# Decoder trunk on one core: two load queues ordered by need at the start, the norm gains on ScalarE's queue, and the last tile's scaling on VectorE

## The chip, the cores and the metric

The kernel runs on one core of one Trainium2 chip. The metric is the time of the device in microseconds (us); lower is better. Engines are named as the profile names them: PE is TensorE, DVE is VectorE, ACT is ScalarE, POOL is GpSimd, SP is SyncE. SP only issues transfers (DMAs); ACT and POOL have queues for transfers of their own.

## What is computed

A decoder trunk of two layers over 512 tokens of width 1024, all in fp32. Layer 0 mixes with a short gated convolution, layer 1 with sliding-window attention; each is followed by a SwiGLU feed-forward part (FFN) of width 2816. Every part ends with a residual update of a normalised result.

```python
def rmsnorm(x, g):
    r = lax.rsqrt(jnp.mean(x * x, axis=-1, keepdims=True) + EPS)
    return (x * r) * g

def short_conv_mixer(h, w_in, conv_w, w_out):
    b_gate, c_gate, u = jnp.split(h @ w_in, 3, axis=-1)
    return (b_gate * causal_depthwise_conv3(c_gate * u, conv_w)) @ w_out

def swiglu(h, w_gate_up, w_down):
    g, u = jnp.split(h @ w_gate_up, 2, axis=-1)
    return (jax.nn.silu(g) * u) @ w_down

# layer 0:  mix = short_conv_mixer(rmsnorm(h, a_pre_norm), w_in, conv_w, w_out)
#           h = h + rmsnorm(mix, a_post_norm)
# layer 1:  mix = window attention of rmsnorm(h, b_pre_norm) @ b_w_q, with k, v of rmsnorm(h, kv_norm)
#           h = h + rmsnorm(mix, b_post_norm)
# both:     h = h + rmsnorm(swiglu(rmsnorm(h, ffn_pre_norm), w_gate_up, w_down), ffn_post_norm)
```

## The kernel before

**Splitting.** TensorE multiplies fp32 numbers as pairs of a high and a low part. ACT copies a tile into its rounded high part (`xhi`, `whi`, `yhi`), DVE subtracts it from the tile for the low part (`xlo`, `wlo`, `ylo`), and each product is three matmuls: high by low, high by high, low by high (`mm3`, L192 to L194). A weight tile is of 128 x 1024; it is loaded by SP into one of seven buffers `raw`, split, and used.

**Order of the work.** Nearly all the work stands in blocks whose order on the engines is written out by hand (`manual_schedule`). The string `CONV` (L37) orders the products of the convolution: `c2 u2 b2` are the three projections of feature tile 2, `P1` to `P7` products of a block scheme for the output, `w0` to `w3` the tiles of the output weights that the closing uses. `in_line` prepares the weights three jobs ahead of their use, and after a job takes steps from a list `late`, the steps that follow a projection on the other engines (L764 to L787). POOL also issues transfers that add blocks of later weights in DRAM (`issue`, L534, tiles `hsum`); each waits for room on POOL's queue, and POOL does its own arithmetic in order with them.

**The start.** `gt` holds all gains that are used as a column per feature, 128 x 64. POOL issues its load (L137). `xt[0]` to `xt[7]` are the transposed input, 128 x 512 each, `first[0]` to `first[2]` the first three weight tiles, which come in three cuts (`CUTS`: feature tiles 0 and 1, then 2 and 3, then 4 to 7) by `piece(queue, t, c)` (L219 to L221). The first two cuts are of 128 KB, the third is of 256 KB, an `xt` of 256 KB. While they come, PE runs ten matmuls on a constant (`idle`). Then ACT does `token_hi(0)` (L674: `xhi` of `xt[0]` times a gain from `gt`) and six pieces of the first weights (`first_hi`, L666), DVE the low parts, and PE the products of feature tile 0 (L686, `pcub`: `products(0, ...)`, nine matmuls with tiles 0, 1, 2 in turn), then those of tiles 1 to 7.

**Close of the convolution.** `close` (L869) makes the output of each of four token tiles in two halves (`pmix`): for tile 0 first all products but the last, and after each half ACT and DVE split two weight tiles of the FFN (`ahead.one()`, L407 and L412). The last product needs the last `yhi` (L775), which comes from the convolution's last projection `b7`. `res` is an `Update` for the norm behind it: `take` adds `pmix` to the tile `mix`, `square_mix` sums the squares on ACT, `mean` makes `uv` on DVE (L292) and `ur`, its power -0.5, on POOL (L296); `scale` multiplies `mix` by the gains `G` (L289, half a tile at a time), and `update` adds it to the residual `h` (L301). Behind it tiles are normalised on ACT (`xn`, L323) and transposed on PE (`xt`, L334). `G` is one row of 1024 gains spread over all partitions, loaded by `res.load` (L253 to L255) on ACT's queue.

**The end.** The loop at L1169 closes the last FFN. The second half of the last token tile is made in two quarters (`take_quarter`, L267): DVE adds `pmix` to `mix` (L270); for the first quarter ACT then sums the squares; for the second DVE adds the sums so far and EPS (`us`, L276), then reduces the quarter's squares into `uv` (L279), and POOL makes `ur` (L283). The first half of `mix` is scaled on POOL, the second on DVE. Two updates of 512 columns each then make the output, with a transfer behind each.

Of the kernel before, what the change touches and what calls it, by code (L numbers as in the profile page):

```python
# [13 lines left out]
ALU = mybir.AluOpType  # L14
# [5 lines left out]
KT = D // P  # L20
# [40 lines left out]
EPS = 1e-6  # L61
# [3 lines left out]
G_FPRE = (24, 32)  # L65
# [3 lines left out]
B_CONV, B_ATT, B_FFN = 0, 1, (2, 3)  # L69
# [3 lines left out]
def yoco_kernel(  # L73
# [22 lines left out]
    nc = tc.nc  # L96
# [39 lines left out]
    gt = const.tile([P, N_GAIN], F32, name="gt")  # L136
    nc.gpsimd.dma_start(gt, gains)  # L137
    ident = const.tile([P, P], F32, name="ident")
# [80 lines left out]
    def piece(queue, t, c):  # L219
        c = slice(CUTS[c][0] * P, CUTS[c][1] * P)  # L220
        queue.dma_start(first[t][:, c], w_in[0, t, :, c])  # L221

    for t in range(3):
        piece(nc.scalar, t, 0)
    nc.sync.dma_start(xt[0], xT[0])
    nc.sync.dma_start(xt[1], xT[1])
    for t in range(2):
        piece(nc.scalar, t, 1)
    nc.sync.dma_start(xt[2], xT[2])
    piece(nc.sync, 2, 1)  # L230
    nc.sync.dma_start(xt[3], xT[3])
# [7 lines left out]
    class Update:  # L239
# [27 lines left out]
        def take_quarter(self, t, c, ps):  # L267

            m = self.mix[t][:, S + c : S + c + 256]
            nc.vector.tensor_tensor(out=m, in0=ps[:, :256], in1=m, op=ALU.add)  # L270
            i = 2 * t
            if not c:
                nc.scalar.activation(self.junk[:, S : S + 256], m, AF.Square, scale=1 / 32,
                                     accum_out=self.s[:, 8:9])
                return
            nc.vector.tensor_scalar(out=self.s[:, i : i + 1], in0=self.s[:, i : i + 1],  # L276
                                    scalar1=self.s[:, 8:9], scalar2=EPS, op0=ALU.add,
                                    op1=ALU.add)
            nc.vector.tensor_tensor_reduce(out=self.junk[:, S : S + 256], in0=m, in1=m,  # L279
                                           scale=1 / D, scalar=self.s[:, i : i + 1],  # L280
                                           op0=ALU.mult, op1=ALU.add,
                                           accum_out=self.v[:, t : t + 1])
            nc.gpsimd.tensor_tensor(out=self.r[:, t : t + 1], in0=self.v[:, t : t + 1],  # L283
                                    in1=mhalf[:, :1], op=ALU.pow)

        def scale(self, t, half, eng=nc.vector):
            c = slice(half * S, (half + 1) * S)
            m = self.mix[t][:, c]
            eng.tensor_tensor(out=m, in0=m, in1=self.G[:, c], op=ALU.mult)  # L289

# [448 lines left out]
    ys, acts, mix_c = [], [], [None] * NB  # L739
    both = []  # L740

    def conv(f, pc=None, pu=None, pb=None):
# [36 lines left out]
        def end():  # L779
            if f >= KT // 2:  # L780
                return [split]
            if f % 2 == 0:
                return []
            p = pair_sums(both[-1], acts)
            return [lambda i=i: (p[i](), p[i + 1]()) for i in (0, 2, 4)]
# [163 lines left out]

    res = Update(mix_c, B_CONV, [G_FPRE[0]])  # L950
    res.leaves = True

    sum_on("o0")
    issue(len(issues))
    ahead = Ahead(first_weights(0))
    with tc.manual_schedule(engines=ALL):
        sum_on("o1")
        issue(len(issues))
        res.load(nc.scalar)
        close(ws, ys, 0, res, ahead)  # L960


    def ffn(l, before, ahead, gain, gpres, following):
# [204 lines left out]
        with tc.manual_schedule(engines=ALL):  # L1168
            for t in range(NB):  # L1169
                for half in range(2):  # L1170
# [8 lines left out]
                    else:  # L1179
# [4 lines left out]
                        if t == NB - 1:  # L1184
                            res.update(t - 1, 0, S)
                            res.scale(t, 0, nc.gpsimd)
                if t < NB - 1:
                    res.scale(t, 0)
                    res.mean(t)
# [404 lines left out]
```

## Time and profile before

| what | value |
|---|---|
| time, median of 3 runs | 1031.55 us (1031.83, 1031.44, 1031.55) |
| time of the profiled execution | 1034.99 us |
| its span in the trace | 1033.2 us |
| PE busy | 1019.7 us, 99% |
| DVE busy | 823.5 us, 80% |
| ACT busy | 576.9 us, 56% |
| POOL busy | 196.7 us, 19% |
| HBM read and written | 237.15 and 102.76 MB, 329 GB/s |

All times inside the kernel come from the one profiled execution, in us from the start of its span. The time of the execution holds 1.8 us more than the span. A row of the timeline gives the start, the length, the engine, the line, the operation with what it writes and reads, how many instructions it joins, and in brackets the idle time ahead of it and what ended that. PE is close to fully busy, so the reading goes to the few places where it stands still or runs at a lower granted clock.

### The profile page before, as it was taken

How to read it: one execution, taken by the hardware profiler on the slowest of the kernel's cores; microseconds unless marked ns; L12 is line 12 of the kernel's file. 1: busy time of each engine (PE TensorE's matmuls, PEld its weight loads, DVE VectorE, ACT ScalarE, POOL GpSimd, SP SyncE). 2: the span in 40 equal slices, each digit the busy share in tenths (PEclk: the TensorE clock that was granted, in tenths of full speed). 3: DMA queues.
4: the chain of work that ended last, by engine and by line, in shares of the span. 5: the costliest groups of instructions: out<-in, count | busy, mean ns of one | idle time of the engine just before them, and what ended most of it. 6: DMA issues, size and time to landing. Idle time of an engine off the chain costs nothing.

```text
span 1033.2 us, 17488 instructions
## 1 busy us (share of the span) xinstructions
PE 1019.7 (99%) x6650; PEld 928.4 (90%) x6650; DVE 823.5 (80%) x1403; ACT 576.9 (56%) x1039; POOL 196.7 (19%) x261
## 2 busy tenths in 40 slices
PE   8999999999999999999999999999999999999997
PEld 7888887999989899999898888889998999989986
DVE  5676657888777978878869998688886788887786
ACT  7232534865655454566466777668565554645632
POOL 0433132102101021000122664221111010210001
PEclk9999999999999999999999999999999999999998
DMA  9797789548978889879503879985899676988732
GB/s 338 282 242 239 187 258 326 170 164 249 315 251 271 269 275 300 282 211 307 196 1 127 220 208 269 265 258 164 257 291 319 182 252 204 315 290 257 249 127 82
DMA packets 66756, 244.59 MB, mean 237 GB/s; under 512 B 7776, under 2 KB 8672, under 8 KB 54896
## 3 DMA queue, kind: packets, MB, share of 16 engines
q1 hardware_dynamic: 51040, 145.52, 38.7%
q0 software_dynamic: 14624, 96.51, 36.5%
q10 hardware_dynamic: 1008, 1.44, 0.4%
q8 instruction: 52, 0.85, 0.3%
q14 instruction: 32, 0.26, 0.1%
HBM read 237.15 MB, written 102.76 MB: 329 GB/s over the span
## 4 chain that ended last, share of the span: by engine, by line
PE 89%; DVE 4%; DMA 4%; ACT 1%; issue 1%; POOL 1%; POOLq 0%; DVEq 0%; ACTq 0%
PE gx L194 7%; PE gx L193 7%; PE gx L192 7%; PE gz L194 4%; PE gz L193 4%; PE gz L192 4%; PE px L193 3%; PE px L192 3%; PE px L194 3%; PE pcub L194 3%; PE pcub L192 3%; PE pcub L193 3%; DMA hsum<-in_w_gb_dram 3%; PE pmix L192 2%; PE pmix L193 2%; PE pmix L194 2%
## 5 line engine op out<-in xcount | busy, mean ns | idle before, releaser
L466 DVE TENSOR_TENSOR wlo<-raw,whi 128x1024 fp32r<-128x1024 f32 x225 | 275.1, 1226 | 93.4 <-ACT whi L465 93.3
L465 ACT ACTIVATE whi<-raw 128x1024 fp32r<-128x1024 f32 x225 | 234.2, 1049 | 120.2 <-DVE raw L453 22.3
L192 PE MATMUL gx<-xt,whi 128*128 128x256 f32 x480 | 135.8, 283 | 0.0
L193 PE MATMUL gx<-xt,whi 128*128 128x256 f32 x480 | 135.8, 283 | 0.0
L194 PE MATMUL gx<-xt,wlo 128*128 128x256 f32 x480 | 135.8, 283 | 0.0
L534 POOL DMA_DIRECT2D hsum<-in_w_gb_dram x96 | 63.4, 728 | 156.3 <-ACT whi L465 82.3
L192 PEld LDWEIGHTS gx<-xt,whi 128*128 128x128 f32 x480 | 92.2, 192 | 0.0
L193 PEld LDWEIGHTS gx<-xt,whi 128*128 128x128 f32 x480 | 92.2, 192 | 0.0
L194 PEld LDWEIGHTS gx<-xt,wlo 128*128 128x128 f32 x480 | 92.2, 192 | 0.0
L534 POOL DMA_DIRECT2D hsum<-hsum x32 | 25.3, 790 | 265.2 <-ACT whi L465 156.0
L1012 ACT ACTIVATE st<-gx 128x256 f32<-128x256 f32 x80 | 30.1, 382 | 81.1 <-PE gx L194 81.0
L193 PE MATMUL pcub<-xhi,whi 128*128 128x512 f32 x168 | 65.4, 389 | 0.0
L192 PE MATMUL pcub<-xlo,whi 128*128 128x512 f32 x168 | 65.4, 389 | 0.0
L194 PE MATMUL pcub<-xhi,wlo 128*128 128x512 f32 x168 | 65.4, 389 | 0.0
L192 PE MATMUL px<-wlo,ahi 128*128 128x512 f32 x120 | 46.7, 389 | 0.0
L193 PE MATMUL px<-whi,ahi 128*128 128x512 f32 x120 | 46.7, 389 | 0.0
L194 PE MATMUL px<-whi,alo 128*128 128x512 f32 x120 | 46.7, 389 | 0.0
L194 PE MATMUL gy<-xhi,wlo 128*128 128x256 f32 x160 | 45.3, 283 | 0.0
L193 PE MATMUL gz<-xt,whi 128*128 128x256 f32 x160 | 45.3, 283 | 0.0
L194 PE MATMUL gx<-xhi,wlo 128*128 128x256 f32 x160 | 45.3, 283 | 0.0
L192 PE MATMUL gy<-xlo,whi 128*128 128x256 f32 x160 | 45.3, 283 | 0.0
L193 PE MATMUL gy<-xhi,whi 128*128 128x256 f32 x160 | 45.3, 283 | 0.0
(270 smaller groups left out, 3123.0 us busy)
## 6 DMA issues: line engine op xcount, KB each, us to landing
hsum<-in_w_gb_dram POOLq DMA_DIRECT2D x96, 512.0 KB, 8.1
raw<-hsum SPq DMA_DIRECT2D x88, 512.0 KB, 7.8
raw<-in_w_gb_dram SPq DMA_DIRECT2D x60, 512.0 KB, 7.8
hsum<-in_w_dn_dram POOLq DMA_DIRECT2D x36, 512.0 KB, 8.6
raw<-in_w_dn_dram SPq DMA_DIRECT2D x32, 512.0 KB, 6.7
hsum<-hsum POOLq DMA_DIRECT2D x28, 512.0 KB, 5.7
raw<-in_w_in_dram SPq DMA_DIRECT2D x21, 512.0 KB, 7.9
hsum<-in_w_dn_dram POOLq DMA_DIRECT2D x12, 768.0 KB, 12.5
```

Of the source, the lines that this page charges most:

```text
L192: nc.tensor.matmul(out, whi, xlo, start=start, stop=False, **kw)
L193: nc.tensor.matmul(out, whi, xhi, start=False, stop=False, **kw)
L194: nc.tensor.matmul(out, wlo, xhi, start=False, stop=stop, **kw)
L465: self.begun = nc.scalar.activation(hi[:, :n], raw, AF.Copy)
L466: nc.vector.tensor_tensor(out=lo[:, :n], in0=raw, in1=hi[:, :n].bitcast(F32), op=ALU.subtract)
L534: nc.gpsimd.dma_start(dst, src, max_dma_last_dim=4 * 4 * S, **kw))
L1012: nc.scalar.activation(s, x, AF.Copy)
```

## The change

Three places are edited.

1. The load of `gt` moves from POOL's queue to the head of ACT's. The loads of the first tiles are issued in another order, and on other queues: ACT keeps `gt` and the first cuts of weight tiles 0 and 1; all the rest is SP's.
2. The `Update` object of the convolution (`res`) is made before the convolution's jobs, and the load of its gains `G` becomes a step in the list `late` behind the split of feature tile 6 (`f == KT - 2`), inside the block of the convolution, in place of the head of the closing's block.
3. In the last FFN's closing, the first half of the last token tile is scaled by DVE behind the second quarter, as the second half already was, and no longer by POOL. In `take_quarter` the small addition for `us` goes ahead of the addition of `pmix` to `mix`.

```diff
--- before.py
+++ after.py
@@ -134,7 +134,6 @@
 
 
     gt = const.tile([P, N_GAIN], F32, name="gt")
-    nc.gpsimd.dma_start(gt, gains)
     ident = const.tile([P, P], F32, name="ident")
     make_identity(nc, ident)
     ones = const.tile([P, P], F32, name="ones")
@@ -220,14 +219,15 @@
         c = slice(CUTS[c][0] * P, CUTS[c][1] * P)
         queue.dma_start(first[t][:, c], w_in[0, t, :, c])
 
+    nc.scalar.dma_start(gt, gains)
+    nc.sync.dma_start(xt[0], xT[0])
+    piece(nc.scalar, 0, 0)
+    piece(nc.sync, 2, 0)
+    piece(nc.scalar, 1, 0)
+    nc.sync.dma_start(xt[1], xT[1])
     for t in range(3):
-        piece(nc.scalar, t, 0)
-    nc.sync.dma_start(xt[0], xT[0])
-    nc.sync.dma_start(xt[1], xT[1])
-    for t in range(2):
-        piece(nc.scalar, t, 1)
+        piece(nc.sync, t, 1)
     nc.sync.dma_start(xt[2], xT[2])
-    piece(nc.sync, 2, 1)
     nc.sync.dma_start(xt[3], xT[3])
     for t in range(3):
         piece(nc.sync, t, 2)
@@ -267,15 +267,16 @@
         def take_quarter(self, t, c, ps):
 
             m = self.mix[t][:, S + c : S + c + 256]
+            i = 2 * t
+            if c:
+                nc.vector.tensor_scalar(out=self.s[:, i : i + 1], in0=self.s[:, i : i + 1],
+                                        scalar1=self.s[:, 8:9], scalar2=EPS, op0=ALU.add,
+                                        op1=ALU.add)
             nc.vector.tensor_tensor(out=m, in0=ps[:, :256], in1=m, op=ALU.add)
-            i = 2 * t
             if not c:
                 nc.scalar.activation(self.junk[:, S : S + 256], m, AF.Square, scale=1 / 32,
                                      accum_out=self.s[:, 8:9])
                 return
-            nc.vector.tensor_scalar(out=self.s[:, i : i + 1], in0=self.s[:, i : i + 1],
-                                    scalar1=self.s[:, 8:9], scalar2=EPS, op0=ALU.add,
-                                    op1=ALU.add)
             nc.vector.tensor_tensor_reduce(out=self.junk[:, S : S + 256], in0=m, in1=m,
                                            scale=1 / D, scalar=self.s[:, i : i + 1],
                                            op0=ALU.mult, op1=ALU.add,
@@ -283,10 +284,10 @@
             nc.gpsimd.tensor_tensor(out=self.r[:, t : t + 1], in0=self.v[:, t : t + 1],
                                     in1=mhalf[:, :1], op=ALU.pow)
 
-        def scale(self, t, half, eng=nc.vector):
+        def scale(self, t, half):
             c = slice(half * S, (half + 1) * S)
             m = self.mix[t][:, c]
-            eng.tensor_tensor(out=m, in0=m, in1=self.G[:, c], op=ALU.mult)
+            nc.vector.tensor_tensor(out=m, in0=m, in1=self.G[:, c], op=ALU.mult)
 
         def mean(self, t):
             nc.vector.tensor_scalar(
@@ -738,6 +739,8 @@
         nc.vector.tensor_scalar(out=nsnk, in0=snk, scalar1=-1.0, scalar2=None, op0=ALU.mult)
     ys, acts, mix_c = [], [], [None] * NB
     both = []
+    res = Update(mix_c, B_CONV, [G_FPRE[0]])
+    res.leaves = True
 
     def conv(f, pc=None, pu=None, pb=None):
 
@@ -778,7 +781,7 @@
 
         def end():
             if f >= KT // 2:
-                return [split]
+                return [split, lambda: res.load(nc.scalar)] if f == KT - 2 else [split]
             if f % 2 == 0:
                 return []
             p = pair_sums(both[-1], acts)
@@ -947,16 +950,12 @@
         return ([w_gu[l, f, j] for f in range(2) for j in range(2)]
                 + [w_gb[l, 0, b] for b in range(2)])
 
-    res = Update(mix_c, B_CONV, [G_FPRE[0]])
-    res.leaves = True
-
     sum_on("o0")
     issue(len(issues))
     ahead = Ahead(first_weights(0))
     with tc.manual_schedule(engines=ALL):
         sum_on("o1")
         issue(len(issues))
-        res.load(nc.scalar)
         close(ws, ys, 0, res, ahead)
 
 
@@ -1183,9 +1182,8 @@
                         res.square_mix(t, half)
                         if t == NB - 1:
                             res.update(t - 1, 0, S)
-                            res.scale(t, 0, nc.gpsimd)
+                res.scale(t, 0)
                 if t < NB - 1:
-                    res.scale(t, 0)
                     res.mean(t)
                 res.scale(t, 1)
                 if t < NB - 2:
```

In the rows below, a name such as `raw_108` is a tile with its buffer number; the numbers differ between the two kernels (`raw_108` before is `raw_107` after: weight tile 0). First, ACT at the start of the program, before:

```order
L221 DMA raw_108<-in_w_in_dram 128x256
L221 DMA raw_109<-in_w_in_dram 128x256
L221 DMA raw_110<-in_w_in_dram 128x256
L221 DMA raw_108<-in_w_in_dram 128x256
L221 DMA raw_109<-in_w_in_dram 128x256
L659 ACT_TABLE_LOAD
L659 ACTIVATE warm_256<-ones 128x1
L674 ACTIVATE xhi_222<-xt_104,gt 128x512
L666 ACTIVATE whi_240<-raw_108 128x128
L666 ACTIVATE whi_242<-raw_109 128x128
L666 ACTIVATE whi_244<-raw_110 128x128
```

The same place of ACT after the change:

```order
L222 DMA gt<-in_gains_dram 128x64
L220 DMA raw_107<-in_w_in_dram 128x256
L220 DMA raw_108<-in_w_in_dram 128x256
L660 ACT_TABLE_LOAD
L660 ACTIVATE warm_256<-ones 128x1
L675 ACTIVATE xhi_222<-xt_103,gt 128x512
L667 ACTIVATE whi_240<-raw_107 128x128
L667 ACTIVATE whi_242<-raw_108 128x128
L667 ACTIVATE whi_244<-raw_109 128x128
```

ACT issues three transfers in place of five ahead of its table load, and the first of them is `gt`. SP's first transfers before (`xt_104` is the pair of `xt[0]` and `xt[1]`, `xt_105` that of `xt[2]` and `xt[3]`):

```order
L225 DMA xt_104<-in_xT_dram 128x512
L226 DMA xt_104<-in_xT_dram 128x512
L229 DMA xt_105<-in_xT_dram 128x512
L221 DMA raw_110<-in_w_in_dram 128x256
L231 DMA xt_105<-in_xT_dram 128x512
L221 DMA raw_108<-in_w_in_dram 128x512
L221 DMA raw_109<-in_w_in_dram 128x512
L221 DMA raw_110<-in_w_in_dram 128x512
```

And after:

```order
L223 DMA xt_103<-in_xT_dram 128x512
L220 DMA raw_109<-in_w_in_dram 128x256
L227 DMA xt_103<-in_xT_dram 128x512
L220 DMA raw_107<-in_w_in_dram 128x256
L220 DMA raw_108<-in_w_in_dram 128x256
L220 DMA raw_109<-in_w_in_dram 128x256
L230 DMA xt_104<-in_xT_dram 128x512
L231 DMA xt_104<-in_xT_dram 128x512
L220 DMA raw_107<-in_w_in_dram 128x512
L220 DMA raw_108<-in_w_in_dram 128x512
```

The first cut of weight tile 2 (`raw_109` after) now stands between `xt[0]` and `xt[1]`, and the second cuts of all three ahead of `xt[2]`.

Second, ACT at the end of the convolution and the start of its closing, before (L181: halves of the output weights `w1` to `w3`; L465: weights of the last job; L775: the `yhi` of feature tiles 6 and 7; L407: the FFN's weights):

```order
L181 ACTIVATE whi_1306<-raw_1190 128x512
L181 ACTIVATE whi_1307<-raw_1190 128x512
L465 ACTIVATE whi_1344<-raw_1192 128x1024
L775 ACTIVATE yhi_1348<-bry_1132 128x512
L181 ACTIVATE whi_1378<-raw_1194 128x512
L181 ACTIVATE whi_1379<-raw_1194 128x512
L181 ACTIVATE whi_1391<-raw_1216 128x512
L181 ACTIVATE whi_1392<-raw_1216 128x512
L255 DMA G_1451<-in_behind_dram 128x1024
L775 ACTIVATE yhi_1429<-bry_1318 128x512
L407 ACTIVATE whi_1465<-raw_1439 128x1024
L407 ACTIVATE whi_1471<-raw_1441 128x1024
```

The same place after:

```order
L778 ACTIVATE yhi_1319<-bry_1135 128x512
L466 ACTIVATE whi_1351<-raw_1195 128x1024
L255 DMA G_1355<-in_behind_dram 128x1024
L180 ACTIVATE whi_1384<-raw_1197 128x512
L408 ACTIVATE whi_1465<-raw_1442 128x1024
L180 ACTIVATE whi_1385<-raw_1197 128x512
L408 ACTIVATE whi_1471<-raw_1444 128x1024
L180 ACTIVATE whi_1397<-raw_1219 128x512
L408 ACTIVATE whi_1486<-raw_1469 128x1024
L180 ACTIVATE whi_1398<-raw_1219 128x512
L408 ACTIVATE whi_1492<-raw_1475 128x1024
L778 ACTIVATE yhi_1435<-bry_1325 128x512
```

The load of `G` passes the halves of the last two output weights, and the four conversions of the FFN's weights (L407 before, L408 after) now stand between those halves, ahead of the last `yhi`. DVE's subtractions behind them move alike. The order of PE's instructions is the same in both kernels.

Third, DVE at the end of the program, before (`mix_8949` is the last token tile):

```order
L259 TENSOR_TENSOR mix_8949<-pmix_11496,mix_8949 128x512
L301 TENSOR_SCALAR h_11384<-mix_8939,ur_11376,h_11384 128x512
L270 TENSOR_TENSOR mix_8949<-pmix_11513,mix_8949 128x256
L301 TENSOR_SCALAR h_11384<-mix_8939,ur_11376,h_11384 128x512
L270 TENSOR_TENSOR mix_8949<-pmix_11530,mix_8949 128x256
L276 TENSOR_SCALAR us_11374<-us_11374 128x1
L279 ISA junk_11378,uv_11375<-mix_8949,us_11374 128x256
L279 ISA uv_11375 128x1
L289 TENSOR_TENSOR mix_8949<-mix_8949,G_11377 128x512
L301 TENSOR_SCALAR h_11386<-mix_8949,ur_11376,h_11386 128x512 x2
```

And after:

```order
L259 TENSOR_TENSOR mix_8949<-pmix_11496,mix_8949 128x512
L302 TENSOR_SCALAR h_11384<-mix_8939,ur_11376,h_11384 128x512
L275 TENSOR_TENSOR mix_8949<-pmix_11512,mix_8949 128x256
L302 TENSOR_SCALAR h_11384<-mix_8939,ur_11376,h_11384 128x512
L272 TENSOR_SCALAR us_11374<-us_11374 128x1
L275 TENSOR_TENSOR mix_8949<-pmix_11529,mix_8949 128x256
L280 ISA junk_11378,uv_11375<-mix_8949,us_11374 128x256
L280 ISA uv_11375 128x1
L290 TENSOR_TENSOR mix_8949<-mix_8949,G_11377 128x512 x2
L302 TENSOR_SCALAR h_11386<-mix_8949,ur_11376,h_11386 128x512 x2
```

The scaling of 128x512 stands twice on DVE, and the addition for `us` (L272 after) stands ahead of the second quarter's `mix`. POOL has one scaling of 128x512 fewer.

## The prediction

> **What bounds the kernel now.** I read the busy times first, then what TensorE (PE) waited for, then the granted clock in short windows, then the three places that the change touches.
>
> ```profile
> PE 1019.7 (99%) x6650; PEld 928.4 (90%) x6650; DVE 823.5 (80%) x1403; ACT 576.9 (56%) x1039; POOL 196.7 (19%) x261
> PE xt L334 <- ACT xn L323: 2.2, 1, 2.2
> PE pcub L686 <- ACT whi L666: 2.0, 1, 2.0
> ```
>
> The first row is the busy time of each engine, the others are PE's waits (total, times, longest). PE is busy for 99% of the span. Apart from its first wait for a constant it stands still twice: 2.0 us before its first real product (`pcub`), and 2.2 us in the closing of the convolution, where the transposes wait for a normalised token tile. An edit can thus save only at PE's start, at that second stop, after PE's last matmul, or where PE runs slowly. The last is seen in windows of 3.41 us (columns: the stretch, its length, busy time of PE, PEld, DVE, ACT, POOL with counts, granted clock, DMA share, GB/s):
>
> ```profile
> 3.96:7.37 3.41, 1.38 (x11) 1.16 (x10) 0.43 (x3) 2.06 (x7) 0.00 (x0) 1.00 1.07 371
> 7.37:10.79 3.42, 3.42 (x10) 2.77 (x9) 3.17 (x10) 3.42 (x10) 0.00 (x0) 0.50 0.94 287
> 178.04:181.45 3.41, 1.41 (x7) 0.89 (x5) 2.61 (x6) 3.35 (x7) 1.12 (x2) 1.00 1.02 425
> 181.46:184.87 3.41, 3.23 (x16) 3.23 (x16) 2.74 (x5) 1.55 (x4) 0.34 (x1) 0.50 0.90 370
> ```
>
> In both places a window with PE busy for only 1.38 or 1.41 us (40%) is followed by one at clock 0.50. So each stop costs twice: the standing still, and half of the next 3.4 us.
>
> **Part 1, the first loads.** ACT converts the first token tile (`xhi`, which needs the gains `gt` and `xt`), then the six first weight tiles; PE follows.
>
> ```profile
> 0.74 2.37 ACTq L221 DMA_DIRECT2D raw<-in_w_in_dram  x5
> 1.29 0.74 POOL L137 DMA_DIRECT2D gt<-in_gains_dram  x1 [0.84 <-POOLq L1583]
> 4.44 0.20 ACT L659 ACTIVATE warm<-ones 128x1 f32<-128x1 f32 x1
> 5.99 0.72 ACT L674 ACTIVATE xhi<-xt,gt 128x512 fp32r<-128x512 f32 x1 [1.34 <-DMA gt<-in_gains_dram]
> 6.61 1.29 ACT L666 ACTIVATE whi<-raw 128x128 fp32r<-128x128 f32 x6
> 6.96 1.32 PE L686 MATMUL pcub<-xhi,whi 128*128 128x512 f32 x3 [2.03 <-ACT whi L666]
> 10.63 0.93 PE L686 MATMUL pcub<-xhi,whi 128*128 128x512 f32 x3
> 12.75 0.84 PE L686 MATMUL pcub<-xhi,whi 128*128 128x512 f32 x3
> ```
>
> And the times from issue to landing (last number) of the first, second and third transfer on the queues:
>
> ```profile
> xt<-in_xT_dram SPq DMA_DIRECT2D x1, 256.0 KB, 3.5
> raw<-in_w_in_dram ACTq DMA_DIRECT2D x1, 128.0 KB, 3.6
> raw<-in_w_in_dram ACTq DMA_DIRECT2D x1, 128.0 KB, 4.6
> xt<-in_xT_dram SPq DMA_DIRECT2D x1, 256.0 KB, 4.9
> raw<-in_w_in_dram ACTq DMA_DIRECT2D x1, 128.0 KB, 5.1
> gt<-in_gains_dram POOLq DMA_DIRECT2D x1, 32.0 KB, 4.7
> ```
>
> ACT is ready at 4.64 and waits until 5.99 for `gt`, which POOL issued at 1.29 and which took 4.7 us. Issued first on ACT's queue at 0.74, `gt` is of 32 KB; the nearest rows are the first transfers of the two queues, 3.5 and 3.6 us, and its own 4.7 us is the other end. That gives 4.2 to 5.4; I take 4.2, the row of the same queue and rank. `xt` lands there too. So `xhi` runs from 4.2 to 4.9, with the table load and `warm` over by then: three issues end near 2.2 in place of 3.1, and 1.28 us of table load and 0.2 follow.
>
> The next thing that ACT needs is not `gt`. It takes the weight tiles in the order 0, 1, 2, and tile 1 is now ACT's third transfer. Before, the third ones landed at 6.5 (SP: 1.65 + 4.9) and 6.7 (ACT: 1.66 + 5.1), with 1152 KB in all (3 x 256 and 3 x 128). Now the three of SP hold 256, 128, 256 KB and those of ACT 32, 128, 128, which is 928 KB. The second pair ended at 5.7 with 768 KB, so by bytes 928 KB are in at 5.7 + (160 / 384) x 1.0 = 6.1. By rank alone it stays at 6.7. I take 6.0 to 6.1, nearer to the bytes. The second weight conversion, which began one fifth of a us after 6.61, at 6.8, then begins at 6.05: **0.8 us earlier**. From there ACT runs without a gap as before, and its later loads do not come later: the two queues carry the same bytes, 32 KB moved apart. On SP's queue the pieces of the second cut now pass `xt[2]` and `xt[3]`; ACT reads them in just that order, the cut first.
>
> The Trainium skill ("DMA: Bandwidth & Descriptors", Queues, rings and completion order) says that a DMA engine takes turns between queues packet by packet; the trace agrees in that equal ranks landed together, 6.5 and 6.7, though one was twice as large. By that rule alone the sum would lose its 0.8 us, which is the third rival below.
>
> PE follows ACT. If the clock still falls to 0.50, PE does its first 18 matmuls at the same slow pace and the whole is 0.8 earlier. If it does not, more is won: before, the eight or so matmuls from 7.6 to 10.6 stood 0.43 us apart, later nine stand from 10.63 to 12.75, 0.23 apart. VectorE's corrections still hold up some of these, so I count 1.5 us for it, with 1.7 (half of 3.41) as its bound. Whether the clock falls: PE now stops from 4.9 to 5.2, does one product, and stops from 5.5 to 6.4; the rest of the window of 3.41 us is busy, some 64%. The rows show 40% as too little and 100% as enough, and nothing between.
>
> The Trainium skill ("TensorE: Matmul & The Clock Gate", Part 1) has the clock fall after a whole idle window of about 3.4 us. The rows above speak against it: 40% busy was already too little. By that rule the new start would run at full clock; it is the case of the first two rivals, and the rows bear it out only as far as its length of window.
>
> **Part 2, the gains `G` and the close of the convolution.** The load of `G` itself saves nothing: the first row is its issue, and of the transfers issued in this stretch (last number of the two rows behind it: from issue to landing) the slowest took 16.3 us, which would still have `G` in by 163.6, before its use near 168.
>
> ```profile
> 147.26 0.33 ACTq L255 DMA_DIRECT2D G<-in_behind_dram  x1
> raw<-in_w_gu_dram SPq DMA_DIRECT2D x1, 512.0 KB, 8.2
> hsum<-in_w_gb_dram POOLq DMA_DIRECT2D x2, 512.0 KB, 16.3
> 158.97 0.69 DVE L770 TENSOR_TENSOR bry<-pcub,rrow 128x512 f32<-128x512 f32 x1 [0.72 <-PE pcub L194]
> 160.42 0.63 ACT L775 ACTIVATE yhi<-bry 128x512 fp32r<-128x512 f32 x1 [10.46 <-DVE bry L771]
> 162.04 4.63 DVE L412 TENSOR_TENSOR wlo<-raw,whi 128x1024 fp32r<-128x1024 f32 x4 [0.26 <-ACT whi L407]
> 168.82 0.21 DVE L292 TENSOR_SCALAR uv<-us 128x1 f32<-128x1 f32 x1
> 168.27 2.28 POOL L534 DMA_DIRECT2D hsum<-in_w_dn_dram  x4
> 170.30 0.86 POOL L296 TENSOR_TENSOR ur<-uv,mhalf 128x1 f32<-128x1 f32 x1
> 181.64 3.41 PE L334 MATMUL xt<-ident,xn 128*128 128x128 f32 x15 [2.19 <-ACT xn L323]
> ```
>
> What does move is the order on ACT and VectorE: the four conversions of the next stage's weights (4.63 us on VectorE) now stand among the last ones of the convolution. The fourth waits until PE has finished product b7 (158.97 is VectorE's start behind it), and the last `yhi` stands behind it on ACT. I put the rows' durations in the new order: conversion 159.0 to 160.05, its correction on VectorE to 161.5, `bry` to 162.1, `yhi` to 162.75 in place of 161.05. PE needs it after 18 products from 158.97, at 163.05, so some 0.3 us of cover are left; I cost it at nothing, and 0.5 us if the cover goes.
>
> In exchange VectorE reaches tile 0 about 2.5 us earlier. That buys nothing by itself: `uv` was ready at 169.03, but POOL computed `ur` only at 170.30, behind its sum transfers. Those are paced by the DMA queue, whose load is the same, so `ur`, the normalised tile and PE's second stop stay where they are with regard to the convolution: 0, with 1.27 us (170.30 less 169.03) of loss or gain as the bound.
>
> **Part 3, the last tile.** POOL's scaling of 1.30 us goes, and one of 0.69 us comes on VectorE.
>
> ```profile
> 1024.64 1.30 POOL L289 TENSOR_TENSOR mix<-mix,G 128x512 f32<-128x512 f32 x1 [1.54 <-ACT junk L264]
> 1023.66 0.74 DVE L301 SCALAR_TENSOR_TENSOR h<-mix,ur,h 128x512 f32<-128x512 f32 x1
> 1024.83 1.66 DVE L301 SCALAR_TENSOR_TENSOR h<-mix,ur,h 128x512 f32<-128x512 f32 x1
> 1025.60 0.28 PE L194 MATMUL pmix<-whi,alo 128*128 128x256 f32 x1
> 1026.40 0.41 DVE L270 TENSOR_TENSOR mix<-pmix,mix 128x256 f32<-128x256 f32 x1
> 1026.97 0.48 DVE L279 CUSTOM_DVE_ANT_0 junk<-mix,us 128x256 f32<-128x256 f32 x1
> 1027.54 1.05 POOL L283 TENSOR_TENSOR ur<-uv,mhalf 128x1 f32<-128x1 f32 x1 [1.61 <-DVE uv L279]
> 1027.50 0.69 DVE L289 TENSOR_TENSOR mix<-mix,G 128x512 f32<-128x512 f32 x1
> 1028.63 1.41 DVE L301 SCALAR_TENSOR_TENSOR h<-mix,ur,h 128x512 f32<-128x512 f32 x2 [0.44 <-POOL ur L283]
> ```
>
> The same update takes 0.74 us alone and 1.66 us while POOL scales. Without POOL it ends at 1025.57, and the last `mix` waits for PE's last matmul instead (1025.60 + 0.28): 1025.95 in place of 1026.40. The sum `us` now stands ahead of `mix`, so the reduction follows at 1026.4 (before: 1026.97). POOL's `ur` runs 0.57 later, from 1026.95 to 1028.0. VectorE meanwhile scales both halves, two starts 0.6 apart from 1026.9, to 1028.1. The final update begins at 1028.1 in place of 1028.63: **0.5 us less**. If the update stays at 1.66 the second scaling costs about 0.1; if `ur` speeds up, nothing more is won, VectorE being the later one. Bounds: 0.1 more to 0.7 less.
>
> **The sum.** 0.8 + 0 + 0.5 = 1.3 us less. The rows come from a profiled execution of 1034.99 us, with a span of 1033.2; the median of the runs shown is 1031.55, and I take the difference off that: **1030.2 us**. With the bounds of these parts it is 1029.2 to 1031.2.
>
> **Rivals.** *The clock holds at the start, the second stop stays as it is:* 0.8 + 1.5 + 0.5 = 2.8 less, 1028.7. For it: 64% against 40% busy. Against it: nothing shows what is enough, and the position of the windows may differ from run to run.
>
> *It holds at both places:* if PE comes 2.3 us earlier and the windows stay where they are, the second stop, of 2.19 us up to 181.64, becomes one from 177.15 to 179.34 and is cut by the window's edge at 178.04 into 0.9 and 1.3 us, 26% and 38% idle, like the start. Then 1.7 more is won: 4.5 less, 1027.0.
>
> *Landing by rank:* tile 1 of the weights still comes at 6.7, and the start gains 0.1. Then 0.6 less, 1031.0.
>
> *Slower:* the fourth conversion also waits for its own load, and that now holds up the convolution's last `yhi`. It has cover until 159.3; before, its own load (8.2 us, issued at 144.35) landed at 152.5, but the two sum transfers issued near 150.2 took 16.3 and came near 166.5. If this load came then, the last `yhi`, 3.75 later (159.0 to 162.75 above), would stand at 170.25 and PE would stop for 7.2 us from 163.05 instead of 2.2 at 179: a loss of 5.0 less the 1.3 is 3.7, 1035.3. It decides only if that load comes 7 us later than it did.
>
> **How the numbers follow.** Chances: forecast 0.42, clock held at the start 0.22, at both 0.16, landing by rank 0.13, slower 0.07. The forecast is the likeliest, not a mean. The range from 1026.8 to 1031.4 takes in the first four and leaves out the fifth and their ends. A measurement of this kernel tells 0.2%, 2.1 us, from no change; the forecast and the landing by rank lie within it, and the two cases of the held clock are faster by more, with a small part of the forecast's own range: faster 0.43, same 0.50, slower 0.07.
>
> **What would show it.** In the profile after, ACT's first `xhi` begins near 4.2 and its second weight conversion near 6.05; PE's first product stands near 5.2. The window that holds the second and third product shows clock 0.50 next or not, which separates the forecast from the first two rivals. In the close, the last `yhi` stands near 162.7 less the gain, PE has no new wait there, and `ur` still follows POOL's transfers. At the end the update is 0.74 long and the final one begins 0.5 us earlier after PE's last matmul. The forecast is wrong if the clock holds, if PE waits for the last `yhi`, or if tile 1 lands at 6.7.

## The result and the profile after

The changed kernel took 1030.49 us (median of 21 executions, 1028.96 to 1033.39), the kernel before, beside it on the same chips, 1033.34 us (21 executions, 1031.33 to 1037.57). The ratio is 0.9974 with a 95% interval of 0.9963 to 0.9985, so 2.7 us less (1.5 to 3.8). Put on the 1031.55 us from which the forecast started, that is 1028.9 us. The forecast was 1030.2, with 1026.8 to 1031.4 as its range: the sign and the range held, the size was about half of what came. A second comparison, of 11 executions with 29, gave 0.9983 (0.9974 to 0.9993), 1.8 us less.

Executions of the same kernel before differ by 6 us among themselves, and a single trace is one of them. So each reading below says of which execution it is, and the three places are read one by one.

**The start, changed kernel.** The timeline of ACT:

```profile
0.75 0.41 ACTq L222 DMA_DIRECT2D gt<-in_gains_dram  x1
3.89 0.72 ACT L675 ACTIVATE xhi<-xt,gt 128x512 fp32r<-128x512 f32 x1 [0.24 <-DMA gt<-in_gains_dram]
4.64 0.31 ACT L667 ACTIVATE whi<-raw 128x128 fp32r<-128x128 f32 x1
6.76 1.11 ACT L667 ACTIVATE whi<-raw 128x128 fp32r<-128x128 f32 x5 [1.82 <-DMA raw<-in_w_in_dram]
```

The third transfers on the two queues, from issue (1.66) to landing in the last column:

```profile
xt<-in_xT_dram SPq DMA_DIRECT2D x1, 256.0 KB, 4.9
raw<-in_w_in_dram ACTq DMA_DIRECT2D x1, 128.0 KB, 5.1
```

The gains arrive early and the first token tile is converted at 3.89 in place of 5.99, 0.3 us sooner than forecast. But the second weight conversion begins at 6.76 (before: 6.8): it now waits for its own tile, and in this execution the third transfers take the same 4.9 and 5.1 us as before. What PE waited for, and PE in three of the clock's windows, two at the start and the one of the second stop (the columns are those of the prediction's windows; no granted clock was recorded before the first rise, at 10.63, and the view shows that time as 1.00):

```profile
PE xt L335 <- ACT xn L324: 2.5, 1, 2.5
PE pcub L687 <- ACT whi L667: 1.0, 1, 1.0
```

```profile
0.39:3.80 3.41, 2.74 (x13) 2.74 (x14) 0.32 (x3) 1.49 (x2) 0.56 (x4) 1.00 0.56 149
3.80:7.21 3.41, 2.41 (x11) 1.90 (x10) 0.40 (x2) 1.48 (x5) 0.00 (x0) 1.00 1.04 304
177.87:181.28 3.41, 1.60 (x8) 1.05 (x6) 2.67 (x7) 2.96 (x7) 0.58 (x2) 1.00 1.02 425
```

The clock's pace is seen in the products. The first row is of this trace, the second of another execution of the same kernel (`e_after`), whose clock had risen at 5.15:

```profile
8.14 1.05 PE L687 MATMUL pcub<-xhi,wlo 128*128 128x512 f32 x2
```

```profile
7.38 0.62 PE L687 MATMUL pcub<-xhi,wlo 128*128 128x512 f32 x2
```

Two matmuls take 1.05 us in the one and 0.62 in the other: the same program runs the start at half clock in one execution and at full clock in the next. In the one, `close` begins at 158.78 us, in the other at 156.88.

**The close of the convolution, changed kernel** (ACT, DVE, POOL and PE):

```profile
161.71 0.63 ACT L778 ACTIVATE yhi<-bry 128x512 fp32r<-128x512 f32 x1 [1.89 <-DVE bry L774]
166.00 0.21 DVE L293 TENSOR_SCALAR uv<-us 128x1 f32<-128x1 f32 x1
166.31 0.80 POOL L535 DMA_DIRECT2D hsum<-in_w_gb_dram  x1 [15.19 <-DMA hsum<-in_w_gb_dram]
168.11 0.79 POOL L535 DMA_DIRECT2D hsum<-in_w_gb_dram  x1 [1.01 <-DMA hsum<-in_w_gb_dram]
168.63 2.28 POOL L535 DMA_DIRECT2D hsum<-in_w_dn_dram  x4
170.65 0.85 POOL L297 TENSOR_TENSOR ur<-uv,mhalf 128x1 f32<-128x1 f32 x1
171.54 1.29 DVE L302 SCALAR_TENSOR_TENSOR h<-mix,ur,h 128x1024 f32<-128x1024 f32 x1 [4.74 <-POOL ur L297]
182.01 1.86 PE L335 MATMUL xt<-ident,xn 128*128 128x128 f32 x15 [2.53 <-ACT xn L324]
```

The last `yhi` comes 1.3 us later (161.71, before 160.42), under PE's cover. `uv` begins 2.8 us earlier (166.00 for 168.82), and DVE then stands for 4.74 us, since POOL's `ur` still comes behind its sum transfers, at 170.65 (before 170.30). The rows of POOL show why: the first two of these wait for the landing of earlier transfers, until 166.31 and 168.11. PE's second stop remains, 2.53 us.

**The end, changed kernel** (DVE, POOL and PE's last matmul):

```profile
1023.62 0.74 DVE L302 SCALAR_TENSOR_TENSOR h<-mix,ur,h 128x512 f32<-128x512 f32 x1
1024.28 0.21 DVE L272 TENSOR_SCALAR us<-us 128x1 f32<-128x1 f32 x1
1024.40 0.28 PE L193 MATMUL pmix<-whi,alo 128*128 128x256 f32 x1
1024.71 0.42 DVE L275 TENSOR_TENSOR mix<-pmix,mix 128x256 f32<-128x256 f32 x1 [0.22 <-PE pmix L193]
1025.58 1.29 DVE L290 TENSOR_TENSOR mix<-mix,G 128x512 f32<-128x512 f32 x2
1025.74 0.93 POOL L284 TENSOR_TENSOR ur<-uv,mhalf 128x1 f32<-128x1 f32 x1 [3.86 <-DVE uv L280]
1026.79 1.41 DVE L302 SCALAR_TENSOR_TENSOR h<-mix,ur,h 128x512 f32<-128x512 f32 x2
```

The update beside which POOL used to scale takes 0.74 us in place of 1.66, the last `mix` waits for PE (0.22), and the final update begins 2.39 us behind the start of PE's last matmul; before it was 1028.63 - 1025.60 = 3.03. From that matmul to the end of the span it is 1031.3 - 1024.4 = 6.9 us, before 1033.2 - 1025.6 = 7.6.

### The profile page after: what moved, and what is told of

Read it like the earlier page. It is cut to its first block, busy times and chain, and to the rows that moved or that the text cites. A ratio compares the mean times of both kernels' runs of the same rounds, so it can differ in the third digit from the quotient of the medians.

```text
span 1031.3 us, 17485 instructions
## 1 busy us (share of the span) xinstructions
PE 1019.1 (99%) x6650; PEld 927.5 (90%) x6650; DVE 822.4 (80%) x1404; ACT 577.6 (56%) x1039; POOL 193.9 (19%) x259
## 4 chain that ended last, share of the span: by engine, by line
PE 89%; DVE 4%; DMA 4%; ACT 1%; POOL 1%; issue 1%; ACTq 0%; DVEq 0%; POOLq 0%
PE gx L193 7%; PE gx L192 7%; PE gx L191 7%; PE gz L193 4%; PE gz L192 4%; PE gz L191 4%; PE px L191 3%; PE px L192 3%; PE px L193 3%; PE pcub L192 3%; PE pcub L193 3%; PE pcub L191 3%; DMA hsum<-in_w_gb_dram 3%; PE pmix L193 2%; PE pmix L192 2%; PE pmix L191 2%
```

## The experiments

Two theories were set against each other: that the parts win what the traces show (the end 0.7 us, the start through a half-clock window that falls more rarely, the close nothing), and that the earlier loads and the earlier VectorE save time in themselves. Each kernel ran 12 times, except the changed kernel again (11) and the last one (5), beside the kernel before. "Close" is the start of PE's first product of the convolution's close, "stop" PE's second stop, "end" the stretch from the start of PE's last matmul to the end of the span, all in us from the one trace of each.

| kernel | ratio to before (95%) | clock up at the start | close | stop | end |
|---|---|---|---|---|---|
| before | 1 | fell at 7.4 | 158.77 | 2.19 | 7.6 |
| `e_before`, before again | 1.0002 (0.9989 to 1.0015) | fell at 8.7 | 159.21 | 1.46 | 7.6 |
| `e_start`, loads alone | 0.9995 (0.9978 to 1.0012) | from 5.55 | 156.79 | 1.41 | 7.6 |
| `e_gains`, `G` alone | 0.9997 (0.9985 to 1.0010) | not before 10.47 | 158.66 | 1.94 | 7.6 |
| `e_tail`, end alone | 0.9987 (0.9975 to 0.9999) | from 4.82 | 156.98 | 1.64 | 7.0 |
| `e_no_gains`, loads and end | 0.9995 (0.9981 to 1.0008) | from 5.21 | 156.53 | 2.5 | 6.9 |
| `e_no_start`, `G` and end | 0.9994 (0.9976 to 1.0012) | not before 9.91 | 158.37 | 0.8 | 7.0 |
| changed | 0.9974 (0.9963 to 0.9985) | not before 10.63 | 158.78 | 2.53 | 6.9 |
| `e_after`, changed again | 0.9983 (0.9974 to 0.9993) | from 5.15 | 156.88 | 2.1 | 6.9 |
| `e_after_warm` | 0.9985 (0.9967 to 1.0003) | from 5.92 | 157.42 | 1.2 | 6.9 |
| `e_cut` | 0.9993 (0.9974 to 1.0013) | from 4.94 | 157.55 | 1.7 | 6.9 |
| `e_before_ur` | 0.9983 (0.9965 to 1.0001) | from 4.58 | 156.93 | 1.1 | 7.6 |
| `e_ur` | 0.9961 (0.9945 to 0.9978) | from 6.19 | 157.14 | none | 6.9 |
| `e_best` | 0.9961 (0.9947 to 0.9975) | from 5.40 | 156.55 | none | 6.9 |

### The parts alone, and the kernel before again

`e_start` has the changed loads in the kernel before:

```diff
-    nc.gpsimd.dma_start(gt, gains)
+    nc.scalar.dma_start(gt, gains)
+    nc.sync.dma_start(xt[0], xT[0])
+    piece(nc.scalar, 0, 0)
+    piece(nc.sync, 2, 0)
...
```

> Only the first loads are reordered (gt first on ScalarE's queue, the rest by need on SP's). Theory 1, landing by rank: the second weight tile's conversion begins near 6.75 us as before (6.8), PE's second product near 7.1, and the whole gains 0.0 to 0.3 us apart from whether a half-clock window falls on the start. Theory 2, the start is where the change gains: the time falls by 1.5 to 2.5 us (ratio about 0.998), with PE's products at 0.23 us apart from the start.

The second weight conversion began at 6.34 and the second product at 6.70, 0.4 us earlier than the first theory had them; the products stood 0.23 us apart, as the second had it. The interval of the time (0.9978 to 1.0012) covers both. In this trace the clock rose at 5.55 and stayed up, and the close began at 156.79; in the trace of the changed kernel, with the same loads, it was not up before 10.63, and the close began at 158.78.

`e_gains` has only the move of `G`, with the order that comes with it:

```diff
+    res = Update(mix_c, B_CONV, [G_FPRE[0]])
...
-                return [split]
+                return [split, lambda: res.load(nc.scalar)] if f == KT - 2 else [split]
...
-        res.load(nc.scalar)
```

> Only the load of G moves into the convolution, with the order of ScalarE and VectorE that comes with it. Theory 1: PE's order and speed up to 179 us are as before, ur still waits for POOL's sum transfers, so 0 us from the order; only the clock behind PE's second stop can differ, by 1.7 us. Theory 2, the earlier VectorE helps: PE's second stop gets shorter than 2.2 us and the time falls by 1 us or more.

No difference was measured, but the interval (0.9985 to 1.0010) does not exclude the 1 us of the second theory. The trace speaks for the first: `uv` began at 165.88, yet `ur` only at 169.99, behind the sum transfers, and the stop was 1.94 us, between the 2.19 and 1.46 of the kernel before.

`e_tail` has only the end:

```diff
-                            res.scale(t, 0, nc.gpsimd)
+                res.scale(t, 0)
                 if t < NB - 1:
-                    res.scale(t, 0)
```

with `us` ahead of the second quarter's `mix`.

> Only the last token tile's scaling goes to VectorE, with the sum moved ahead. Both theories: from PE's last matmul to the issue of the last output transfer 3.85 us in place of 4.48, so 0.6 us less, whatever the rest does (ratio 0.9994); within the noise of the whole time.

The end measured 7.0 us in place of 7.6 (lines like those above). The whole time was 0.13% less, 0.01 to 0.25%, which holds the 0.06% that the end accounts for.

`e_before` is the kernel before without an edit.

> The kernel before, unchanged, for a second trace and the mean granted clock of its single executions. Theory 1 (the clock decides): most executions show a mean clock of 0.994 to 0.997, one or two half-clock windows more than the changed kernel, whose executions show 0.998 or 0.999 in 16 of 21; ratio 1.000. Theory 2 (steady gain, the clock is chance in both): the mean clocks are spread as those of the changed kernel.

Seven of its 12 executions showed a mean clock of 0.995 to 0.997, as the first theory has it; of the 99 executions of that kernel that ran beside the experiments it was 32, a third and not most. The changed kernel had 6 in 32. The mean only counts from the clock's first record on, so a start that never rose is not in it; and it takes in the half clock that stands at the end of every trace, for 3.6 to 7.3 us. This count is a weak witness. The windows of single traces are a stronger one. In order: the window of PE's first stop in `e_before` and in `e_tail`, the windows of both stops in `e_after`, and the window of the second stop in `e_no_gains`:

```profile
5.26:8.67 3.41, 1.66 (x9) 1.14 (x8) 1.36 (x4) 2.32 (x8) 0.00 (x0) 1.00 1.03 362
```

```profile
4.82:8.23 3.41, 2.14 (x12) 1.57 (x11) 1.36 (x4) 2.59 (x9) 0.00 (x0) 1.00 1.02 352
```

```profile
5.15:8.56 3.41, 2.32 (x11) 1.65 (x11) 1.52 (x5) 2.11 (x8) 0.00 (x0) 1.00 0.94 291
175.82:179.23 3.41, 1.74 (x9) 1.14 (x7) 2.67 (x6) 3.28 (x7) 0.90 (x2) 1.00 1.01 420
```

```profile
175.87:179.28 3.41, 1.34 (x7) 0.82 (x5) 2.67 (x7) 3.23 (x7) 0.85 (x2) 1.00 1.01 422
```

The first and the last were followed by half clock, the others were not. `e_before` and `e_tail` run the same start, with the windows' edges at 5.26 and at 4.82, and the close begins at 159.21 in the one and at 156.98 in the other. Not all of that is the clock, since the loads came later too: PE's first product stands at 7.30 and at 6.61. Three pairs of traces in which the products begin alike, within 0.07 us, give the price of a lost window alone: `e_gains` and `e_tail` (the close at 158.66 and 156.98), `e_no_start` and `e_before_ur` (158.37 and 156.93), the changed kernel and `e_ur` (158.78 and 157.14). It is 1.4 to 1.7 us.

The clock was lost in two ways. In the two traces of the kernel before it had risen, and fell behind the stop. In `e_gains`, `e_no_start` and the changed kernel it had not risen when the stop came. For the first way the new loads help. The window of the first stop, where the clock was up, in `e_start`, `e_no_gains` and `e_ur`:

```profile
5.55:8.96 3.41, 2.63 (x12) 1.81 (x11) 2.02 (x5) 2.62 (x10) 0.00 (x0) 1.00 0.95 291
```

```profile
5.21:8.62 3.41, 2.71 (x13) 1.96 (x12) 1.97 (x6) 2.53 (x9) 0.00 (x0) 1.00 0.97 260
```

```profile
6.19:9.60 3.41, 2.54 (x11) 2.00 (x12) 2.30 (x7) 2.90 (x10) 0.00 (x0) 1.00 0.94 254
```

With `e_after` that is 2.32 to 2.71 us busy in four traces of the new loads, and the clock held in all. With the old loads it is 1.38 (before), 1.66, 2.05 (`e_before_ur`, 4.58 to 7.99) and 2.14, and it fell behind the first two. The second way stays open to the new loads, as the changed kernel's own trace shows.

### All but one part, and the change again

`e_no_gains` and `e_no_start` leave out one of the parts above; `e_after` is the changed kernel.

> The changed kernel once more, beside two kernels that lack one part each. Theory 1 (the parts add up as the traces show them: the end 0.7 us, the start 0.5 us on average by a rarer half-clock window, the close nothing): ratio to before 0.9985 to 0.999. Theory 2 (the parts together win more than apart, as the first comparison's 2.7 us suggests): ratio 0.997 to 0.998. In its trace the closing's first product stands at 156.8 to 157.6 us if the clock held at the start, near 158.8 if not.

> Start and end as changed, G loaded at the head of the close as before. Theory 1 (the move of G is worth nothing while ur waits for POOL's transfers): the same as the changed kernel within 0.05%. Theory 2 (VectorE's earlier arrival at tile 0 is worth about 1 us): slower than the changed kernel by 0.1%.

> G and end as changed, first loads as before. Theory 1: the end alone remains, 0.7 us, and the half-clock window at the start falls as often as before (in 3 of the 5 traces of that start so far): ratio 0.9993, slower than the changed kernel by 0.05%. Theory 2 (the start is the main part): ratio 0.9995 to 1, slower than the changed kernel by 0.15 to 0.25%.

The three intervals overlap; 0.9983, 0.9995 and 0.9994 cannot be told apart, and 0.9983 lies between what the two theories named. The single parts' ratios (0.9995, 0.9997, 0.9987) add up to 0.21% less, the whole gave 0.26% and 0.17%. So the times speak for no gain beyond the sum, and they leave open whether the move of `G` is worth anything between 0 and 1 us; in the traces it is worth nothing up to the end of the second stop (22.5 and 22.4 us from the start of the close, averaged below).

### More matmuls on the constant

```diff
-WARM = 10
+WARM = 17
```

> The changed kernel with 17 in place of 10 matmuls on the constant ahead of the first product, so that PE is busy until the second weight tile has come. Theory 1 (the start's cost is a half-clock window): PE is busy over 80% from 1.06 us on wherever the windows lie, the clock rises by 7.4 us at the latest and stays up; the closing's first product stands at 156.5 to 157.5 us, never near 158.8, and the time is about 0.5 us (a quarter of the executions times 1.8) below the changed kernel's: ratio to before 0.9965 to 0.9975. Theory 2 (only the arrival of the weights counts): the extra matmuls save nothing, and may hold up the first products by up to 1 us.

The close began at 157.42, as the first theory says, and the wait for the first weights was gone. But the ratio, 0.9985, is not below the changed kernel's, though its interval (0.9967 to 1.0003) does not exclude that. The extra matmuls ran until 7.4 us, the first product stood at 7.18, and the close began 0.3 to 0.9 us later than in the traces of the new loads in which the clock held with ten matmuls (156.53 to 157.14). In this trace, then, the later products cost part of what a surer clock can win.

### Smaller first pieces

`e_cut` halves the first cut's bytes:

```diff
+    PIECES = [(0, 1), (1, 4), (4, KT)]
...
-        c = slice(CUTS[c][0] * P, CUTS[c][1] * P)
+        c = slice(PIECES[c][0] * P, PIECES[c][1] * P)
```

> The changed kernel with the first cut of the first three weight tiles reduced to one feature tile (64 KB in place of 128 KB), the second taking the rest (192 KB). Theory 1, transfers land by rank on their queue: ScalarE's second weight conversion still begins at 6.5 to 6.8 us, and the second cut's conversions somewhat later than before, so no gain. Theory 2, they land by bytes: 736 KB in place of 928 KB are ahead of it, and it begins near 5.7 to 6.0 us; PE's first stop is under 0.5 us and the time 0.8 us less.

The third transfer of ACT's queue, and the conversion that waits for it:

```profile
raw<-in_w_in_dram ACTq DMA_DIRECT2D x1, 64.0 KB, 4.9
```

```profile
6.54 1.13 ACT L668 ACTIVATE whi<-raw 128x128 fp32r<-128x128 f32 x4 [1.76 <-DMA raw<-in_w_in_dram]
```

With 64 KB in place of 128, and 736 KB in all in place of 928, it took 4.9 us in place of 5.1, and the conversion began at 6.54. By bytes it would have been 5.7 to 6.0. So this trace speaks for landing by rank. It is one trace: with 128 KB the same transfer took 4.4 to 5.1 us in the seven other traces of the new loads, and the conversion began at 6.09 to 6.76.

### Sum transfers behind `ur`

The six sum transfers at the head of the close are issued by POOL behind the power of token tile 0:

```diff
-        sum_on("o1")
-        issue(len(issues))
-        close(ws, ys, 0, res, ahead)
+        close(ws, ys, 0, res, ahead, lambda: (sum_on("o1"), issue(len(issues))))
...
                 tile_done(res, t, square=t < NB - 2)
+                if t == 0 and then:
+                    then()
```

In the changed kernel:

> The changed kernel with the six sum transfers of the closing issued by POOL behind the power (ur) of token tile 0 in place of ahead of it. Theory 1, POOL's transfers pace the close: ur begins near 166.3 us in place of 170.65, the residual update follows at 167.3, and PE's second stop of about 2 us goes: 2.0 to 2.5 us less than the changed kernel, ratio to before 0.995 to 0.9955. Theory 2, the normalised tile waits for something else (the products of the tiles, ScalarE): the stop stays above 1 us.

```profile
164.34 0.21 DVE L293 TENSOR_SCALAR uv<-us 128x1 f32<-128x1 f32 x1
164.63 0.95 POOL L297 TENSOR_TENSOR ur<-uv,mhalf 128x1 f32<-128x1 f32 x1 [15.15 <-DVE uv L293]
165.55 1.65 POOL L535 DMA_DIRECT2D hsum<-in_w_gb_dram  x2
177.55 1.91 PE L335 MATMUL xt<-ident,xn 128*128 128x128 f32 x16
684.41 1.86 PE L335 MATMUL xt<-ident,xn 128*128 128x128 f32 x15 [1.30 <-ACT xn L324]
```

`ur` now waits for `uv` and not for transfers, and the 16 transposes run without a stop (fourth row). That shows the cause of the second stop: POOL's transfers in front of its own arithmetic. The fifth row shows what became late next: the close of the attention, without such a stop in the changed kernel, stops for 1.30 us in the same way (`uv` begins at 670.97, `ur` at 673.07, behind a sum transfer issued at 672.53). So a part of the gain was given back in this trace. The ratio, 0.9961, is short of the 0.995 to 0.9955 that the first theory named, though its interval (0.9945 to 0.9978) holds it.

In the kernel before:

> The same move of the six sum transfers in the kernel before. Theory 1: uv is ready at 169.0 us there (166.2 in the changed kernel), so ur comes only 1.1 us earlier, at 169.2, and PE's second stop shrinks from 2.2 to about 1 us: ratio 0.9985 to 0.999. Theory 2, the order in which VectorE comes to tile 0 does not matter: it gains as much here as in the changed kernel, 2 to 2.5 us.

```profile
166.97 0.21 DVE L292 TENSOR_SCALAR uv<-us 128x1 f32<-128x1 f32 x1
167.27 0.95 POOL L296 TENSOR_TENSOR ur<-uv,mhalf 128x1 f32<-128x1 f32 x1 [18.23 <-DVE uv L292]
178.71 1.86 PE L334 MATMUL xt<-ident,xn 128*128 128x128 f32 x15 [1.11 <-ACT xn L323]
```

Here `uv` itself is late, 10.0 us behind the start of the close in place of 7.2 (164.34 - 157.14 in `e_ur`), and 1.1 us of the stop remain. So the move of `G` does bring VectorE to tile 0 in time, but the stop shows it only once POOL is free. The time, 0.9983, lies between the two theories, and its interval (0.9965 to 1.0001) holds both.

### Both closes

`e_best` does the same in the attention's close, with `WARM = 14`:

```diff
-                if op in "RH":
+                if op in "RH" and i <= KT:
                     issue(len(issues) // 2 if op == "R" else len(issues))
-            sum_on(f"a{i + 1}")
+            if i <= KT:
+                sum_on(f"a{i + 1}")
...
-        close(rest_w, at, EARLY, res, ahead)
+        close(rest_w, at, EARLY, res, ahead, lambda: sum_on(f"a{KT + 2}"))
```

> The changed kernel with the closing's sum transfers behind ur of tile 0, in the convolution and likewise in the attention (its last two behind that ur), and with 14 matmuls on the constant in place of 10. If POOL's transfers pace both closes and the start costs by its clock: no stop above 0.7 us is left in the convolution's close, the one of 1.3 us in the attention's close is gone or below 0.5, the clock is up by 7.1 us and stays; 1.3 us less than with the convolution's alone: ratio to before 0.994 to 0.9955. If another wait takes the place of the one in the attention, 0.996 as with the convolution's alone.

PE's waits and, of POOL, the attention's close:

```profile
PE idle L663 <- DVE ones L140: 1.1, 1, 1.1
PE psc L1283 <- DVE nm L1295: 0.6, 2, 0.3
```

```profile
670.70 0.94 POOL L297 TENSOR_TENSOR ur<-uv,mhalf 128x1 f32<-128x1 f32 x1 [8.96 <-DVE uv L293]
671.61 1.66 POOL L535 DMA_DIRECT2D hsum<-in_w_dn_dram  x2
```

Neither stop is left, in the convolution or in the attention, and no wait for the first weights. The median is 1028.04 us, the fastest of all kernels here, and the five executions lie within 0.9 us (1027.79 to 1028.70), where the kernel before spreads over 9.5 us beside them. The ratio, 0.9961 (0.9947 to 0.9975), is that of `e_ur`, which ran in another comparison; that the attention's part and the matmuls add 1.3 us to it isn't shown by the times.

## Why the prediction was half right

**The start.** The step that failed is "if the clock still falls to 0.50 ... the whole is 0.8 earlier". Both halves of it did. *The landing:* the second weight conversion was put at 6.05, "nearer to the bytes". In five traces of the new loads (changed, `e_after`, `e_start`, `e_no_gains`, `e_ur`) it began at 6.76, 6.45, 6.34, 6.09 and 6.70, on average 6.47. And the 6.8 from which the gain was counted was one execution; six traces of the old loads average 6.64. The term of 0.8 was 0.2. The rival by rank, with 0.1, was nearer, and `e_cut` points the same way; why two traces (`e_no_gains`, and `e_best` with 6.10) came near to the forecast's 6.05 is open. The Trainium skill ("DMA: Bandwidth & Descriptors", Queues, rings and completion order) has a DMA engine take turns between queues packet by packet; the trace of `e_cut` fits it, 4.9 us for 64 KB against 5.1 for 128 in the changed kernel.

*The clock:* in four of those five traces it held through the start, and the close began at 156.53 to 157.14; in the fifth at 158.78. With the old loads it held in two of six (156.93 and 156.98), and was lost in four (158.37 to 159.21). Averaged, 158.15 against 157.22: 0.9 us. Of this 0.2 us is the landing; the rest is the price of a lost window, 1.4 to 1.7 us, times how much rarer it was. One lost in five against four in six could be chance by itself; that the windows with the stop are fuller with the new loads (2.32 to 2.71 us busy, against 1.38 to 2.14) is the reason to expect it. The forecast saw the mechanism, and knew that 64% busy lay between what it had seen fall and hold. It then took one of the two as what happens, where executions of one kernel do either. The Trainium skill ("TensorE: Matmul & The Clock Gate", Part 1) calls the window free-running; the traces agree, with edges at 3.96, 5.26 and 4.82 in three executions of one start. Its other rule, a fall after a whole idle window, would have had no execution fall at the start; 1.66 us busy of 3.41 was followed by half clock in `e_before`.

**The close.** Right, with its reason: 0 us, since `ur` follows POOL's transfers. The last `yhi` had 0.4 us more cover than forecast (161.71 + 0.63 = 162.34 in place of 162.75), `uv` came 2.8 us earlier (forecast 2.5), PE got no new wait. Over the eleven traces in which POOL's transfers stand ahead of `ur`, leaving out those of `e_before_ur`, `e_ur` and `e_best`, from the start of the close to the end of the second stop, the old order took 22.5 us on average and the new one 22.4. The forecast gave no value to what `uv` makes possible; `e_ur` shows it.

**The end.** Right in its steps, 0.7 us in place of 0.5. Counted from the start of PE's last matmul, DVE's two scalings began at 1.18 us, not at 1.3, and the final update at 2.39, not at 2.5; what follows it was another 0.06 us shorter.

**The sum** by the traces is 0.9 + 0 + 0.7 = 1.6 us, against 2.7 (1.5 to 3.8) and 1.8 (0.7 to 2.7) measured. Both intervals hold 1.6; whether there is more, up to the 2.7, isn't settled. A half-clock window behind the second stop (1.5 us: the 15 transposes took 3.41 us in it, 1.86 at full clock) stood in two of the five traces with the old order of the close (before, `e_no_gains`) and in none of the six with the new order and a stop; eleven traces cannot tell that from chance.

**The rivals.** The held clock at the start (22%) was nearest to what happens, without its 0.8 of earlier weights. The slower case did not come near: the fourth conversion ran at 158.75 behind PE's product, not behind its load.

## What to carry to other kernels

Where PE waits for one or two us and a window of 3.4 us can fall on it, the price of the stop is a lottery with one ticket per execution: count it as the chance that a window is lost, times its price (here 1.4 to 1.7 us), from several traces, not from one. Before moving a load forward, ask what the next operation behind it waits for; here the gains were in use 2.1 us earlier, and the second weight tile 0.2. And an engine that both issues transfers and computes a small value on the path should compute first: with POOL's transfers behind it the changed kernel's stop of 2.53 us was gone, and its ratio was 0.9961. In the kernel before the same move gave 0.9983, as the whole change did in its second comparison, though there with an interval that reaches no change.

## What the runs showed of the hardware

In the 3.41 us windows of these traces the clock rose after 2.90 us busy (before, 0.55 to 3.96) and more, and not after 2.74 or less (changed kernel, above). It fell after 1.34, 1.38 and 1.41 us, and in `e_before` after 1.66; it held after 1.60 (changed kernel), 1.66 (`e_gains`, 177.73 to 181.14, around the second stop), 1.74 (`e_after`) and all above. So a share that keeps the clock up does not raise it, and near 1.6 us the busy time alone doesn't decide. A transfer of 64 KB (`e_cut`) and one of 128 KB (changed kernel), third on the same queue, took the same time within 0.2 us, while the one of 128 KB varied by 0.7 us between traces of the same loads. An update of 128x512 on DVE took 1.66 us beside a scaling on POOL, and 0.74 without it.
